# Output projection of layer 0 as seven half products per pair of column tiles, sums of weights added by DMA

## The chip, the cores and the metric

The kernel runs on one core of a Trainium2 chip. The metric is the device time of one execution in microseconds (us). Three runs of the kernel before are shown, and one further execution of it was taken by the hardware profiler; the profile and the trace quoted below are of that one.

## The reference

A trunk of two layers over 512 tokens and 16 meta tokens (528 in all, T in the code), width 2048, all in float32. Layer 0 is grouped-query attention, layer 1 gated linear attention. Each layer is `h <- h + post_norm(mixer(pre_norm(h)))`, with RMS norms over the width. What the change touches is the end of layer 0's mixer, then its post-norm and residual:

```
o = ...                                    # (528, 2048): 16 heads of 128
y = (o * silu(gate)) @ w_out               # 2048 x 2048: the output projection
h = h + rmsnorm(y, post_norm[0])
u = rmsnorm(h, pre_norm[1])                # input of layer 1's projections
```

## The kernel before

**Layout and precision.** Activations lie feature-major: a tile is 128 features by 528 tokens, `uh[:, k]` and `ul[:, k]` for k in 0..15. Every float32 operand is split in two parts: `split` (L130) makes the high part by a copy on ScalarE (ACT) and the rest by a subtraction on VectorE (DVE). A product of weights and activations is three matmuls, high*high, high*low and low*high (`three`, L153). Weights come by `weights` (L143): one DMA on SyncE's queue (SP) of 128 x 1024 elements into one of two buffers `wraw`, then the split into one of three pairs `whi`, `wlo`.

**Output projection of layer 0.** The gated heads `og` were written to DRAM (`og_d`) while attention ran; `reload` (L542) brings them back, splits them into `uh`, `ul`, and multiplies the last two by their gates. The first two column tiles run side by side with k outermost (`group`, L171), because heads arrive one by one; the other 14 run in `project` (L158, called at L682): 16 values of k for the first half of the tokens (264), then 16 for the second. That is 16 column tiles x 2 halves x 16 k x 3 = 1536 matmuls of 264 columns.

**What follows a tile.** `squares` (L601) lets ACT copy the result from PSUM to SBUF, scaled by the post-norm's weight, into `hs[m]`, which stays in SBUF, and square it; GpSimd (POOL) adds the square to `acc`. After the last tile `mean_rsqrt` (L618) makes the norm `r0` by a matmul with ones, for each half of the tokens. `residual` (L625) then forms the new `h` from `hs[k]`, `r0` and the old `h` (from DRAM, `h0_d`), and splits it into `uh`, `ul` for layer 1. The first half's norm is ready while the second half of the last tile still runs, so the residual starts before the projection ends. The first group of layer 1 (`group` with `low_rank`, L649) takes k as the residual delivers it.

**What sets the order.** The program is recorded through a scheduler; `tc.high_priority(n)` moves an instruction up. Each engine runs its own queue strictly in order. A tile from a pool with a given number of buffers waits until the last reader of the buffer's former tile is done, and the wait stands in the queue of the engine that writes it, in front of everything behind it.

Of the kernel before, what the change touches and what calls it, by code (L numbers as in the profile page):

```python
# [19 lines left out]
P = 128  # L20
# [14 lines left out]
AHEAD = 400  # L35
SLOTS = (2.8, 3.5, 3.5, 3.5, 3.5, 3.5, 3.5, 2.6)


class Clock:
    """Order of emission: main steps advance the time, events run when it has come."""  # L40
# [42 lines left out]
def hybrid_encoder(  # L83
# [37 lines left out]
    def col(i):  # L121
        return cols[:, i:i + 1]
# [3 lines left out]
    # the activations of both layers and their gated outputs, feature-major, in two parts  # L126
# [31 lines left out]
    def project(src, c0, parts, evac, last_k=None):  # L158
        """One column tile of a projection: all of k for one part of the tokens, then for the next."""
# [11 lines left out]
    def group(srcs, accs, extra, ahead=AHEAD, halves=0, units=None):  # L171
        """Several column tiles side by side, k outermost; the first of k by halves of the tokens, if asked."""
# [15 lines left out]

    w_in0 = attn_w_in[0].rearrange("(k p) n -> p k n", p=P)
# [5 lines left out]
    # ======== layer 0: attention ========  # L195
# [156 lines left out]
    # per-token sums of squares: the norm as a column, and along the tokens  # L352
# [182 lines left out]
    slots.append(wa.tile([P, T], F32, tag="vt", name="ogr", bufs=1))  # L535
    NS = len(slots)

    def load_og(k):
        if k < 14:
            nc.sync.dma_start(out=slots[k % NS], in_=og_d[k])  # L540

    def reload(k):  # L542
        if k < 14:
            og = slots[k % NS]
        else:
            if k == 14:
                clk.finish(att)
            og = o_sb[k - 14]
            V.tensor_tensor(og, og, last_gs[k - 14], op=ALU.mult)
        split(uh[:, k], ul[:, k], og)  # L550
        load_og(k + NS)

    for k in range(NS):
        load_og(k)
    EARLY = 4
    last_gs.append(gate(15, lambda k: reload(k - 10) if 10 <= k < 10 + EARLY else None))

    accs0, banks0 = [], []
    for m in range(2):
        for j, (a, b) in enumerate(HALVES):  # L560
            ps = (ps_t.tile([P, 512], F32, tag="t", name="po") if m and j else
                  ps_p.tile([P, 512], F32, tag="pp", name="pp"))[:, :b - a]
            accs0.append((ps, 0, m * P, a, b))
            banks0.append((m, ps, a, b))
# [3 lines left out]
    r1row = c1.tile([P, T], F32, name="r1row")  # L568
# [4 lines left out]
    qf = c1.tile([P, 2, SEQ], F32, name="qf")  # L573

# [1 line left out]
    tr = ExitStack()  # L576
    tp = pool(tr, "tp")
    t2 = pool(tr, "t2", 2)
    hs = [tp.tile([P, T], F32, name=f"h{k}") for k in range(KT)]
    acc = tp.tile([P, T], F32, name="acc")  # L580
    r0 = tp.tile([P, T], F32, name="r0")
    # low-rank gate weights: the down-projection as columns [f hi, b hi, f lo, b lo] from multiples of 32,
    # the up-projections as rows [hi, lo, hi] against the inputs' rows [hi, hi, lo]
# [17 lines left out]
    def squares(m, ps, a, b):  # L601
        A.activation(hs[m][:, a:b], ps, AF.Copy, scale=col(POST + m))
        if m == 0:
            A.activation(acc[:, a:b], ps, AF.Square)
            return
        sq = t2.tile([P, 512], F32, tag="sq", name="sq")[:, :b - a]
        A.activation(sq, ps, AF.Square)
        if m < KT - 1:
            G.tensor_tensor(acc[:, a:b], acc[:, a:b], sq, op=ALU.add)
        return sq  # L610

    for m, ps, a, b in banks0:
        squares(m, ps, a, b)
    ps0.close()
    ps_g = pool(tr, "ps_g1", space=PSUM)
    ps_t = pool(tr, "ps_t1", space=PSUM)

    def mean_rsqrt(row, parts, a, b):  # L618
        ps = ps_t.tile([P, 512], F32, tag="t", name="ssq")[:, :b - a]
        for i, p in enumerate(parts):  # L620
            PE.matmul(ps, ones, p, start=(i == 0), stop=(i == len(parts) - 1))
        V.tensor_scalar(row[:, a:b], ps, 1.0 / D, EPS, op0=ALU.mult, op1=ALU.add)
        rsqrt_inplace(row[:, a:b])

    def residual(k, a, b):  # L625
        if a == 0:
            h0s[k] = t2.tile([P, T], F32, tag="h0", name="h0", bufs=6)
            nc.sync.dma_start(out=h0s[k], in_=h0_d[k])
        h, hi = hs[k][:, a:b], uh[:, k, a:b]
        V.tensor_tensor(h, h, r0[:, a:b], op=ALU.mult)  # L630
        (G if k % 2 else V).tensor_tensor(h, h, h0s[k][:, a:b], op=ALU.add)
# [439 lines left out]
```

## Time and profile before

| | |
|---|---|
| Time, three runs | 1827.38 us median (1826.25 to 1829.39) |
| Span of the profiled execution, first to last instruction | 1825.2 us |
| Median time less that span (start and end around it) | 2.2 us |
| TensorE matmul (PE) busy | 1784.4 us, 98% |
| VectorE (DVE), ScalarE (ACT), GpSimd (POOL) busy | 56%, 49%, 11% |
| Mean granted TensorE clock | 0.995 of full speed |
| Moved by DMA | 184.22 MB |

The profile's page gives the span by engine, by time slices, the chain of work that ended last, and groups of instructions by source line with their count and mean time. The trace can be asked for one tile or one stretch of time. "PE idle" below always means that TensorE had no matmul under way. The output projection takes about 755 to 943 us of the span; the residual with the first group of layer 1 lies from 940 to 1000 us.

### The profile page before, as it was taken

The numbers are of one execution on the slowest core, as the hardware profiler recorded it, in microseconds if no ns is written. First come the engines' busy times: TensorE is split into PE (matmuls) and PEld (weight loads), VectorE is DVE, ScalarE is ACT, GpSimd is POOL, SyncE is SP. The second block draws the span as 40 slices with busy tenths as digits, with TensorE's granted clock in tenths as the row PEclk, the third lists the DMA queues.
The fourth block names the chain that finished last, engine by engine and source line by source line (L and its number), as shares of the span: only waits on it lengthen the run. The fifth ranks groups of instructions, "written<-read, shape, count | busy, mean of one in ns | idle before, by whom it ended". The sixth has DMA issues, their size and how long they took to land.

```text
span 1825.2 us, 31789 instructions
## 1 busy us (share of the span) xinstructions
PE 1784.4 (98%) x12825; PEld 1683.3 (92%) x12825; DVE 1014.2 (56%) x1941; ACT 892.9 (49%) x1835; POOL 202.5 (11%) x212
## 2 busy tenths in 40 slices
PE   8899999999999999999987999999999999999997
PEld 7899999999999999999987898998999899988886
DVE  5776665656565657622258475656456555654224
ACT  5555444454454544533245586556447455743221
POOL 2211111111111110211137000000000000000000
PEclk9999999999999999999998999999999999999999
DMA  8323232333223242633335323232232323434323
GB/s 266 106 59 82 82 88 85 93 85 88 83 87 93 81 120 76 185 93 93 93 88 163 87 72 89 83 82 82 81 93 80 84 87 92 134 116 172 94 92 127
DMA packets 264595, 184.22 MB, mean 101 GB/s; under 512 B 8108, under 2 KB 240112, under 8 KB 263920
## 3 DMA queue, kind: packets, MB, share of 16 engines
q1 hardware_dynamic: 259808, 165.78, 31.5%
q0 software_dynamic: 4640, 16.42, 2.5%
q8 instruction: 100, 1.64, 0.4%
q14 instruction: 47, 0.39, 0.1%
HBM read 156.03 MB, written 19.64 MB: 96 GB/s over the span
## 4 chain that ended last, share of the span: by engine, by line
PE 92%; DVE 3%; ACT 1%; DMA 1%; POOL 1%; issue 1%; SPq 0%; DVEq 0%; POOLq 0%; ACTq 0%
PE pp L154 22%; PE pp L156 22%; PE pp L155 22%; PE f L985 2%; PE f L983 2%; PE f L984 2%; PE pT L453 2%; PE s L434 1%; PE s L435 1%; PE s L436 1%; PE o L863 1%; PE o L862 1%; PE o L861 1%; PE o L474 1%; PE o L473 1%
## 5 line engine op out<-in xcount | busy, mean ns | idle before, releaser
L154 PE MATMUL pp<-uh,whi 128*128 128x264 f32 (+1 forms) x3072 | 927.4, 302 | 2.5 <-ACT uh L308 2.1
L156 PE MATMUL pp<-uh,wlo 128*128 128x264 f32 (+1 forms) x3072 | 916.4, 298 | 0.0
L155 PE MATMUL pp<-ul,whi 128*128 128x264 f32 (+1 forms) x3072 | 915.1, 298 | 0.7 <-DVE ul L309 0.7
L154 PEld LDWEIGHTS pp<-uh,whi 128*128 128x128 f32 x3072 | 578.5, 188 | 21.1 <-ACT uh L308 2.5
L155 PEld LDWEIGHTS pp<-ul,whi 128*128 128x128 f32 x3072 | 578.8, 188 | 16.9 <-DVE ul L309 1.2
L156 PEld LDWEIGHTS pp<-uh,wlo 128*128 128x128 f32 x3072 | 578.5, 188 | 16.2
L132 DVE TENSOR_TENSOR wlo<-wraw,whi 128x1024 fp32r<-128x1024 f32 x256 | 316.0, 1235 | 385.8 <-ACT whi L131 380.7
L131 ACT CAST whi<-wraw 128x1024 fp32r<-128x1024 f32 x256 | 267.7, 1047 | 416.1 <-PE pp L155 297.1
L443 ACT ACTIVATE pn<-s,mx 128x528 f32<-128x528 f32 (+1 forms) x72 | 50.4, 699 | 88.4 <-DVE mx L440 65.0
L985 PE MATMUL f<-whi,ul 128*128 128x512 f32 x192 | 75.6, 394 | 0.0
L983 PE MATMUL f<-whi,uh 128*128 128x512 f32 x192 | 75.5, 393 | 0.0
L984 PE MATMUL f<-wlo,uh 128*128 128x512 f32 x192 | 75.3, 392 | 0.0
L225 POOL TENSOR_TENSOR qw<-qw,cos 128x528 f32<-128x528 f32 x24 | 31.9, 1328 | 372.2 <-DMA qs<-qw 347.7
L888 POOL DMA_DIRECT2D og_d<-og x24 | 12.9, 545 | 486.8 <-DVE og L886 486.8
L439 DVE TENSOR_REDUCE mx<-s 128x1 f32<-128x528 f32 (+1 forms) x72 | 50.8, 705 | 18.5 <-PE s L436 17.3
L235 DVE TENSOR_TENSOR qw<-qw,qs 128x528 f32<-128x528 f32 x24 | 17.0, 708 | 60.0 <-POOL qs L226 60.0
L458 DVE TENSOR_TENSOR pl<-pT,ph 128x512 fp32r<-128x512 f32 (+1 forms) x80 | 47.4, 593 | 4.8 <-ACT ph L457 3.8
L457 ACT CAST ph<-pT 128x512 fp32r<-128x512 f32 (+1 forms) x80 | 40.7, 508 | 16.5 <-PE pT L453 10.4
L428 POOL TENSOR_TENSOR gs<-gs,gr 128x528 f32<-128x528 f32 x16 | 21.2, 1323 | 222.3 <-ACT gs L141 205.4
L984 PEld LDWEIGHTS f<-wlo,uh 128*128 128x128 f32 x192 | 36.1, 188 | 8.3
L985 PEld LDWEIGHTS f<-whi,ul 128*128 128x128 f32 x192 | 36.1, 188 | 8.3
L983 PEld LDWEIGHTS f<-whi,uh 128*128 128x128 f32 x192 | 36.1, 188 | 8.1
(306 smaller groups left out, 2743.2 us busy)
## 6 DMA issues: line engine op xcount, KB each, us to landing
wraw<-in_gla_w_in_dram SPq DMA_DIRECT2D x96, 512.0 KB, 3.9
wraw<-in_attn_w_in_dram SPq DMA_DIRECT2D x95, 512.0 KB, 4.1
wraw<-in_attn_w_out_dram SPq DMA_DIRECT2D x32, 512.0 KB, 3.9
wraw<-in_gla_w_out_dram SPq DMA_DIRECT2D x32, 512.0 KB, 3.8
qs<-qw SPq DMA_DIRECT2D x96, 66.0 KB, 3.0
h<-h_d SPq DMA_DIRECT2D x16, 264.0 KB, 3.8
h_d<-h POOLq DMA_DIRECT2D x16, 256.0 KB, 2.9
h_d<-hb SPq DMA_DIRECT2D x16, 256.0 KB, 3.1
```

The lines of the kernel that those rows point to most:

```text
L131: A.copy(hi, src)
L132: V.tensor_tensor(lo, src, hi.bitcast(F32), op=ALU.subtract)
L154: PE.matmul(ps, wh, uh[:, k, a:b], start=first, stop=False)
L155: PE.matmul(ps, wh, ul[:, k, a:b], start=False, stop=False)
L156: PE.matmul(ps, wl, uh[:, k, a:b], start=False, stop=last)
L439: V.reduce_max(mx, s, axis=AX.XY)
L443: A.activation(pn[:, :T].rearrange("p (a b) -> p a b", a=2), s, AF.Exp, bias=mx, scale=SCALE, accum_out=sm)
L457: A.copy(ph[:, :, c:c + m], pt[:, :, qc:qc + m])
L458: V.tensor_tensor(pl[:, :, c:c + m], pt[:, :, qc:qc + m], ph[:, :, c:c + m].bitcast(F32), op=ALU.subtract)
L983: PE.matmul(ps, uh[:, k, ts], wh[:, kk], start=(k == 0), stop=False)
L984: PE.matmul(ps, uh[:, k, ts], wl[:, kk], start=False, stop=False)
L985: PE.matmul(ps, ul[:, k, ts], wh[:, kk], start=False, stop=(k == KT - 1))
```

## The change

Column tiles are taken in pairs. With the weights of a pair as a 2 x 2 block matrix (A: column tile by half of k, 8 tiles each) and the activations as one (B: half of k by half of the tokens), the eight half products of a pair become seven, each of 8 values of k and 264 tokens (`product`). Numbers of the products are P1 to P7 in `pair_products`.

- **Sums of weights.** `Pair` loads four 128 x 1024 blocks by SP. Four more blocks are added onto the loaded ones by accumulating DMAs that POOL issues (`accum_op=ALU.add`): `chain` is A21, then A21+A22 for P5, then +A11 for P6, then +A12 for P3; `a11` becomes A11+A21 for P7. `chain` and `a11` have six buffers `sraw` together.
- **Sums of activations.** `sums_of(j)`, for 8 values of j, reloads two heads (`o1`, `o2`) from `og_d`, forms four sums on POOL (`d0` to `d3` in the built program) and splits five blocks. `o1` and `o2` share two buffers; each `d` has one.
- **Order.** P1 of the pairs 0 to 3 comes first, on the first half of tokens, then P2 of these pairs beside the sums, then the rest pair by pair: five products for the pairs 0 to 3, seven for 4 to 7.
- **Output.** The pieces of y are combined by DVE, squared by ACT, the squares added by POOL, and each piece of 128 x 264 is written to DRAM (`y_d`) by a DMA that POOL issues. `residual` loads `hs[k]` back from `y_d` (10 buffers) and multiplies by the post-norm's weight itself.
- **Moved.** The small weights of layer 1 (`wr`, `ur`, `wl`, `ups`) were prepared at the projection's start and are now prepared at its end; the first six loads of `h0_d` too.

The diff, cut to its core:

```
+    def split_neg(hi, lo, src):
+        A.activation(hi, src, AF.Copy, scale=-1.0)
+        V.scalar_tensor_tensor(lo, src, -1.0, hi.bitcast(F32), op0=ALU.mult, op1=ALU.subtract)
...
+    class Pair:
+        def __init__(self, src, c0, rawp, ahead=2 * AHEAD):
+            def load(i, j, t, q=nc.sync, **kw):
+                c = c0 + i * P
+                q.dma_start(out=t.rearrange("p (k n) -> p k n", n=P), in_=src[:, 8 * j:8 * j + 8, c:c + P], **kw)
+            def add(i, j, t):
+                with tc.high_priority(ahead):
+                    load(i, j, t, G, accum_op=ALU.add)
...
+                self.chain, self.a11 = [rawp.tile([P, 1024], F32, tag="sraw", name="sraw", bufs=RAWS) for _ in range(2)]
+                self.a12, self.a22 = [wpool.tile([P, 1024], F32, tag="wraw", name="wraw", bufs=2) for _ in range(2)]
+                load(1, 0, self.chain)
+                load(0, 0, self.a11)
+                load(0, 1, self.a12)
+                load(1, 1, self.a22)
+                load(1, 1, self.chain, G, accum_op=ALU.add)
+        def weights(self, n):
+            if n == 7:
+                self.add(1, 0, self.a11)
+            if n == 6:
+                self.add(0, 0, self.chain)
+            if n == 3:
+                self.add(0, 1, self.chain)
+            return split_w({1: self.a11, 7: self.a11, 2: self.a12, 4: self.a22}.get(n, self.chain))
+    def product(w, u):
+        (wh, wl), (bh, bl) = w, u
+        ps = ps_p.tile([P, 512], F32, tag="pp", name="pp")[:, :HALF]
+        for k in range(8):
+            PE.matmul(ps, wh[:, k], bh[:, k], start=(k == 0), stop=False)
+            PE.matmul(ps, wh[:, k], bl[:, k], start=False, stop=False)
+            PE.matmul(ps, wl[:, k], bh[:, k], start=False, stop=(k == 7))
...
-    group([(w_out0, 0, 256)], accs0, lambda k, _: reload(k) if k >= EARLY else None)
...
-    for m in range(2, KT):
-        project(w_out0, m * P, HALVES, evac)
...
+    so2 = pool(so, "so2", 2, side="right")
+    def sums_of(j):
+        o1 = so2.tile([P, T], F32, tag="og", name="o1")
+        o2 = so2.tile([P, T], F32, tag="og", name="o2")
+        nc.sync.dma_start(out=o1, in_=og_d[j])
+        nc.sync.dma_start(out=o2, in_=og_d[j + 8])
+        (b11, b12), (b21, b22) = [[o[:, a:b] for a, b in HALVES] for o in (o1, o2)]
+        d1, d2, d3, d4 = [so2.tile([P, HALF], F32, tag=f"d{i}", name=f"d{i}", bufs=1) for i in range(4)]
+        G.tensor_tensor(d1, b12, b11, op=ALU.subtract)
+        G.tensor_tensor(d2, d1, b22, op=ALU.subtract)
+        G.tensor_tensor(d3, b22, b12, op=ALU.subtract)
+        G.tensor_tensor(d4, d2, b21, op=ALU.add)
+        split(B22[0][:, j], B22[1][:, j], b22)
+        split_neg(T1[0][:, j], T1[1][:, j], d1)
+        split(T2[0][:, j], T2[1][:, j], d2)
+        split(T3[0][:, j], T3[1][:, j], d3)
+        split_neg(T4[0][:, j], T4[1][:, j], d4)
...
+    def done(m, j, first=False, last=None):
...
+            A.activation(sq, y, AF.Square)
+            G.tensor_tensor(acc[:, a:b], acc[:, a:b], sq, op=ALU.add)
...
+        nc.gpsimd.dma_start(out=y_d[m][:, a:b], in_=y)
...
+            hs[k] = t2.tile([P, T], F32, tag="hk", name="hk", bufs=10)
+            nc.sync.dma_start(out=hs[k], in_=y_d[k])
...
-        V.tensor_tensor(h, h, r0[:, a:b], op=ALU.mult)
+        V.scalar_tensor_tensor(h, h, col(POST + k), r0[:, a:b], op0=ALU.mult, op1=ALU.mult)
...
+    def pair_products(i, last):
+        pr = Pair(w_out0, 2 * i * P, so2)
+        if i >= NX:
+            take_p1(i, product(pr.weights(1), B11))
+            take_c11(i, product(pr.weights(2), B21))
+        u2, u3, u4, p5 = [so2.tile([P, HALF], F32, tag=f"u{n}", name=f"u{n}", bufs=1) for n in (2, 3, 4, 5)]
+        A.copy(p5, product(pr.weights(5), T1))
+        V.tensor_tensor(u2, product(pr.weights(6), T2), p1s[i], op=ALU.add)
+        V.tensor_tensor(u4, u2, p5, op=ALU.add)
+        ps = product(pr.weights(7), T3)
...
+        ps = product(pr.weights(4), T4)
...
+        ps = product(pr.weights(3), B22)
```

**Where instructions moved.** First GpSimd's queue at the projection's start. Names: `gs` is the last head's gate, `wr`, `wl`, `ur`, `lr`, `ups` the small weights of layer 1, `acc` the sum of squares. Before:

```order
L428 TENSOR_TENSOR gs_9492<-gs_9492,gr_9367 128x528
L585 DMA wr_9786<-in_gla_w_in_dram 128x16x32
L587 MEMSET wl_9788 128x2048
L591 DMA ur_9794<-in_gla_gk_up_dram 16x2x1024
L593 MEMSET lr0_9757 80x528
L593 MEMSET lr1_9758 80x528
L593 MEMSET ups_9759 80x2048
L609 TENSOR_TENSOR acc_9784<-acc_9784,sq_9810 128x264
```

The same place now, from the last of six accumulating DMAs (`sraw` from the weights) on; `sraw_10001` is the chain of pair 0, `y` a piece of the output, and `d0` to `d3` the four sums, with a new set of numbers for each j:

```order
L214 DMA sraw_10372<-in_attn_w_out_dram 128x8x128
L707 DMA y_d_9653<-y_9746 128x264
L659 TENSOR_TENSOR d0_9697<-o1_9693 128x264
L707 DMA y_d_9653<-y_9823 128x264
L660 TENSOR_TENSOR d1_9698<-d0_9697,o2_9694 128x264
L661 TENSOR_TENSOR d2_9699<-o2_9694,o1_9693 128x264
L662 TENSOR_TENSOR d3_9700<-d1_9698,o2_9694 128x264
L214 DMA sraw_10001<-in_attn_w_out_dram 128x8x128
L659 TENSOR_TENSOR d0_9752<-o1_9748 128x264
L707 DMA y_d_9653<-y_9900 128x264
L707 DMA y_d_9653<-y_9977 128x264
L660 TENSOR_TENSOR d1_9753<-d0_9752,o2_9749 128x264
```

The small weights left this place; accumulating DMAs, stores and sums share one queue. The accumulation of A11 onto pair 0's chain stands between the sums of j = 0 and j = 1.

Second, SyncE's queue in the same stage (`h0` is the old h, `ogr` a reloaded head). Before:

```order
L149 DMA wraw_9684<-in_attn_w_out_dram 128x4x256
L540 DMA ogr_9357<-og_d_70 128x528
L540 DMA ogr_9358<-og_d_70 128x528
L149 DMA wraw_9832<-in_attn_w_out_dram 128x8x128
L540 DMA ogr_9359<-og_d_70 128x528
L540 DMA ogr_9360<-og_d_70 128x528
L149 DMA wraw_9838<-in_attn_w_out_dram 128x8x128
L628 DMA h0_11461<-h0_d_69 128x528
```

Now, with `o1`, `o2` of j = 0 to 3 and the raw weights between them:

```order
L655 DMA o1_9693<-og_d_70 128x528
L656 DMA o2_9694<-og_d_70 128x528
L214 DMA wraw_10003<-in_attn_w_out_dram 128x8x128
L655 DMA o1_9748<-og_d_70 128x528
L214 DMA wraw_10004<-in_attn_w_out_dram 128x8x128
L214 DMA wraw_10186<-in_attn_w_out_dram 128x8x128
L656 DMA o2_9749<-og_d_70 128x528
L214 DMA wraw_10187<-in_attn_w_out_dram 128x8x128
L655 DMA o1_9770<-og_d_70 128x528
L214 DMA sraw_10558<-in_attn_w_out_dram 128x8x128
L656 DMA o2_9771<-og_d_70 128x528
L655 DMA o1_9825<-og_d_70 128x528
```

In the built program each `o1` waits for `d2` of the j before it, and each `o2` for `d3` of the j before it.

Third, GpSimd's queue later in the projection, where before it held nothing but these:

```order
L609 TENSOR_TENSOR acc_9784<-acc_9784,sq_9894 128x264
L609 TENSOR_TENSOR acc_9784<-acc_9784,sq_9947 128x264
L609 TENSOR_TENSOR acc_9784<-acc_9784,sq_10012 128x264
L609 TENSOR_TENSOR acc_9784<-acc_9784,sq_10065 128x264
L609 TENSOR_TENSOR acc_9784<-acc_9784,sq_10130 128x264
```

Now, around the end of pair 1 (`sraw_10184` its chain) and the start of pair 2 (`sraw_10371` its chain; `sraw_10745` is the chain of pair 4):

```order
L214 DMA sraw_10184<-in_attn_w_out_dram 128x8x128
L214 DMA sraw_10745<-in_attn_w_out_dram 128x8x128
L707 DMA y_d_9653<-y_10290 128x264
L702 TENSOR_TENSOR acc_9639<-acc_9639,sq_10292 128x264
L702 TENSOR_TENSOR acc_9639<-acc_9639,sq_10327 128x264
L214 DMA sraw_10371<-in_attn_w_out_dram 128x8x128
L707 DMA y_d_9653<-y_10325 128x264
```

A store and two additions now stand ahead of the DMA that adds A11 onto pair 2's chain.

More of the change, by code (lines that the diff above doesn't have):

```diff
@@ L35 @@
 AHEAD = 400
+RAWS = 6
 SLOTS = (2.8, 3.5, 3.5, 3.5, 3.5, 3.5, 3.5, 2.6)
@@ L558, in hybrid_encoder @@
[L558 to L564, printed above, removed]
-    group([(w_out0, 0, 256)], accs0, lambda k, _: reload(k) if k >= EARLY else None)
-    l0.close()
+        load_a(k)
+    last_gs.append(gate(15, lambda k: reload_a(k - 2) if 2 <= k < 10 else None))
@@ new lines, in hybrid_encoder, with piece, take_p1, take_c11 @@
+    p1s, ys = {}, {}
+    def piece():
+        return so2.tile([P, HALF], F32, tag="y", name="y", bufs=NX + 6)
+    def take_p1(i, ps):
+        p1s[i] = so2.tile([P, HALF], F32, tag="p1", name="p1", bufs=NX)
+        A.copy(p1s[i], ps)
+    def take_c11(i, ps):
+        ys[2 * i, 0] = piece()
+        V.tensor_tensor(ys[2 * i, 0], ps, p1s[i], op=ALU.add)
+    todo0 = list(range(8))
+    for i in range(3):
+        take_p1(i, early[i])
+    for i in range(3, NX):
+        take_p1(i, product(half_weights(2 * i, 0), B11))
+        sums_of(todo0.pop(0))
```

177 lines of the change are left out of this document (109 added, 68 removed).

## The prediction

> **What bounds the kernel now.** First the page: busy time by engine, and the chain of work that ended last.
>
> ```profile
> PE 1784.4 (98%) x12825; PEld 1683.3 (92%) x12825; DVE 1014.2 (56%) x1941; ACT 892.9 (49%) x1835; POOL 202.5 (11%) x212
> ...
> PE 92%; DVE 3%; ACT 1%; DMA 1%; POOL 1%; issue 1%; SPq 0%; DVEq 0%; POOLq 0%; ACTq 0%
> ```
>
> TensorE is the bound nearly everywhere, and GpSimd is the emptiest engine. Next, windows of 20 us inside the output projection and of 5 us in the residual behind it; the columns are named in the first row, clock and DMA share last.
>
> ```profile
> core 0: us, PE busy (x) PEld busy (x) DVE busy (x) ACT busy (x) POOL busy (x), PEclk, DMA share, GB/s
> 780.00:800.00 20.00, 20.00 (x167) 20.00 (x166) 3.12 (x4) 6.37 (x13) 4.11 (x5) 1.00 0.28 80
> ...
> 950.00:955.00 5.00, 2.73 (x19) 2.17 (x17) 5.00 (x9) 3.21 (x8) 3.57 (x5) 1.00 0.28 69
> ...
> 990.00:995.00 5.00, 1.97 (x9) 1.76 (x10) 5.00 (x4) 3.13 (x6) 4.53 (x4) 0.69 0.09 26
> 995.00:1000.00 5.00, 5.00 (x30) 5.00 (x29) 3.27 (x3) 2.27 (x4) 4.39 (x6) 0.63 0.56 152
> 1000.00:1005.00 5.00, 5.00 (x44) 5.00 (x43) 0.00 (x0) 1.18 (x2) 0.00 (x0) 1.00 0.66 194
> ```
>
> In the projection PE never stops: 167 matmuls of 264 columns in 20 us, 0.1198 us each, while every other engine and the DMA are mostly idle. In the residual DVE is full and PE waits. Last, the two ends of the stage in the timeline: the evacuation of the last gate, and the last matmul of the projection with the first one on layer 1's data.
>
> ```profile
> 755.37 0.43 DVE L425 TENSOR_TENSOR gr<-pp,rrow 128x264 f32<-128x264 f32 x1
> ...
> 939.96 0.78 DVE L630 TENSOR_TENSOR h<-h,r 128x264 f32<-128x264 f32 x2 [0.95 <-ACT r L136]
> ...
> 942.29 0.28 PE L156 MATMUL pp<-uh,wlo 128*128 128x264 f32 x1
> 942.70 0.39 PE L652 MATMUL plr<-uh,wl 128*128 128x264 f32 x1
> ```
>
> The projection has PE for itself from 755.3 to 942.6, and layer 1 follows without a gap, because the residual (L630) begins 2.6 us before the projection ends.
>
> **The matmuls removed.** Eight pairs x 7 products x 8 k x 3 are 1344 matmuls instead of 1536, all still 128 x 128 by 264. 192 x 0.1198 = **23.0 us saved**, since PE is never idle here. One product takes 24 x 0.1198 = 2.88 us.
>
> **The sums of activations.** The rows for this part: GpSimd's 264-column addition, its DMA issues, the load of a head, and the weight split with its load.
>
> ```profile
> L609 POOL TENSOR_TENSOR acc<-acc,sq x28: 742/757/1131, 780.5 to 931.7; 128x264 f32<-128x264 f32 x28
> ...
> 759.02 1.32 POOL L428 TENSOR_TENSOR gs<-gs,gr 128x528 f32<-128x528 f32 x1 [11.76 <-ACT gs L141]
> ...
> L525 POOL DMA_DIRECT2D og_d<-o_sb x14 | 8.2, 583 | 14.6 <-DVE o_sb L524 7.3 <-DVE sm L444 6.3 <-DVE pl L458 1.0
> L585 POOL DMA_DIRECT2D wr<-in_gla_w_in_dram x1 | 1.2, 1216 | 0.0
> L149 POOL DMA_DIRECT2D wraw<-in_attn_w_in_dram x1 | 0.8, 806 | 0.0
> ...
> L540 SPq DMA_DIRECT2D ogr<-og_d x14: 319/320/386, 648.6 to 759.1; - x14
> ...
> DMA to landing us min/median/max: 2.7/4.1/5.7
> ...
> L131 ACT CAST whi<-wraw x32: 1037/1047/1048, 755.1 to 939.8; 128x1024 fp32r<-128x1024 f32 x32
> L132 DVE TENSOR_TENSOR wlo<-wraw,whi x31: 1219/1226/1227, 756.3 to 931.0; 128x1024 fp32r<-128x1024 f32 x31
> L149 SPq DMA_DIRECT2D wraw<-in_attn_w_out_dram x28: 367/368/383, 757.6 to 917.6; - x28
> ...
> DMA to landing us min/median/max: 3.6/3.9/5.6
> ...
> wr<-in_gla_w_in_dram POOLq DMA_DIRECT2D x1, 256.0 KB, 5.2
> h<-h_d POOLq DMA_DIRECT2D x4, 1024.0 KB, 8.2
> h_d<-h POOLq DMA_DIRECT2D x16, 256.0 KB, 2.9
> ```
>
> The eight P1 and P2 that run beside the sums last 23.0 us, to 755.3 + 23.0 = 778.3. The sums form a chain: `o2` of one j may load only when `d3` of the j before has read its buffer; then `d1`, `d2`, `d3` follow on GpSimd. One link is 2.7 to 4.1 us of landing (I take 3.4, since SP carries little else then), 3 x 0.76, and 0.2 for two semaphores: 5.9 us. GpSimd alone needs 4 x 0.76 = 3.0 us for each j, 24 us for eight, so the 23 us of cover would not do even without loads.
>
> Step by step. GpSimd finishes the last gate's store at 763.8 and then issues six accumulating DMAs. Their issue I put at 0.9 us, between 0.81 and 1.22 of the two rows with short runs. `o1`, `o2` of j = 0 stand behind the weights of the last P2, which wait for the split of the P2 two before: P1 of pair 3 ends at 766.8, its copy and that split end at 769.5, the heads land at 774.3. `d3` of j = 0 ends at 777.7. Then GpSimd adds A11 onto pair 0's chain; an accumulating DMA is not in the trace, and I take 5.2 us to landing as in the `wr` row, also a GpSimd load of many short runs (bounds 3.9, the same block loaded by SP, and 8.2, the longest GpSimd load): 783.8. GpSimd's next accumulation waits for the split of that chain (2.3 us) and so does the rest of j = 1, whose `d3` ends at 787.8. A raw load and its accumulation stand before j = 2: 794.5. Four links of 5.9 give 818.1 for j = 6; `o2` of j = 7 lands at 821.6, its T2 is split at 823.2. P5, P6 and P7 of pair 0 take each k as it comes (PE's queue interleaves them), and T3 of j = 7 waits behind the split for P3: P7 ends at 826.8. Without waits it would end at 778.3 + 8.6 = 786.9: **40 us lost**. With 2.7 us for each load and 3.9 for the accumulation it is 33, with 4.1 and 8.2 and additions at 0.95 it is 49; none of the links can fall away, so a gain is excluded.
>
> **The accumulations of the later pairs.** P6 uses the chain after A11 was added, which may start only when the split for P5 has read it, and that needs a weight buffer freed three products before P5. From there: split 2.3 us, issue 0.9, landing 5.2, split 2.3 and 0.1 are 10.8; PE arrives at the first low part after three products and two matmuls, 8.9. So each pair waits landing - 3.3 = 1.9 us, and pairs 1 to 7 lose 13.3. In pairs 2 and 3 a store (0.55) and two additions (1.5) stand ahead in GpSimd's queue, some 1.6 us more each. For P3's accumulation there are, from P6's third matmul to P3's, 8.6 - 0.9 - 2.3 = 5.4 us to land, so it is hidden at 5.2. **16.5 us lost**; at a landing of 3.9 it is 7.4, at 8.2 it is 37.5 and P3 adds 2.8 x 7: 57.
>
> On this price the Trainium skill speaks, DMA: Bandwidth & Descriptors, section "Anatomy of one DMA": a GpSimd-issued DMA takes about 2.0 us plus its bytes over 436 GB/s. By it 512 KB land in an estimated 3.2 us, the links above would all but hide, and the sum would be some 14 us lower. The rows above (5.2 us for 256 KB, 8.2 for 1 MB) are slower than that rule; it is the second rival.
>
> Of other work, splits and pieces stay hidden: seven splits of 1.05 us on ACT and 1.23 on DVE in 20.2 us. If all eight blocks and stores of a pair (4.7 MB) moved at 288 GB/s, what queue 1's 165.78 MB in 31.5% of the span amounts to, they would take 16 us against 14.4 to 20.2; here too a slow accumulation would bind.
>
> ```profile
> q1 hardware_dynamic: 259808, 165.78, 31.5%
> ```
>
> **The end of the projection.** Rows: the small weights prepared by ACT and DVE, and the norm.
>
> ```profile
> L594 ACT CAST ups<-ur 16x2048 fp32r<-16x2048 f32 x1 | 1.9, 1909 | 0.0
> L596 DVE TENSOR_TENSOR ups<-ur,ups 16x2048 fp32r<-16x2048 f32 x1 | 2.3, 2282 | 0.7 <-ACT ups L594 0.7
> L622 DVE TENSOR_SCALAR r<-ssq 128x264 f32<-128x264 f32 x2 | 0.9, 426 | 6.4 <-PE ssq L621 6.4
> ```
>
> The first `hs[k]` is no longer in SBUF. Its load waits in SP's queue for the store of P4's last piece: 0.45 (DVE) + 0.55 (issue) + 2.9 (landing) + 3.4 (load) = 7.3 us after P4, 4.4 after P3, where before the residual began 2.6 us ahead of the end. That is 7 us later, and DVE's stage behind it is as long as before: two weight splits (2.5) come earlier, `ups` (2.3) comes in. ACT's two copies of 1.9 us stand around the first residual tiles, 0 to 2 us. **8 us lost**, 5 if the load has landed early, 14 if the later loads from `y_d`, behind the stores of `hb` (layer 1's transposed copy of h), keep DVE waiting.
>
> **The clock.** Rows 990 to 1000 show 0.69 and 0.63 granted once PE is mostly idle, and 1.00 again 5 us later. The sums leave PE idle for four fifths of 48 us, so some 5 us behind them run at about 0.65: **2 us** (0 to 4). The Trainium skill, TensorE: Matmul & The Clock Gate, section "Part 1", says that an idle window of about 3.4 us halves the clock until another 3.4 us were busy; by that it is an estimated 1.7 us, and the rows agree in kind.
>
> **Sum.** -23.0 + 40 + 16.5 + 8 + 2 = +43.5 us. On the span of 1825.2 that gives 1868.7, and with the 2.2 us around it, which the median of the runs shows, **1871 us**. All low ends give 1850, all high ends 1928.
>
> **Rivals.**
> - *Sums covered (faster).* If loads of the next j overlapped GpSimd's work and GpSimd kept pace with PE, the sums would cost nothing: -23.0 + 7.4 + 8 = -7.6, 1820 us. It decides at a link of 2.9 us; GpSimd's four operations alone take 3.0, and the waits in the built program put the load into each link. For it speaks only that the trace shows no GpSimd this busy. 5%.
> - *Accumulations no dearer than a load.* At the 3.9 us of the same block loaded by SP the pairs lose 7.4 instead of 16.5 us and the sums 1.3 less: 1861 us. For it speaks that both move the same 1024 short runs, against it the slower GpSimd rows. 17%. The rule of the Trainium skill named above (DMA: Bandwidth & Descriptors) would make it some 4 us less still.
> - *Slow accumulations.* If adding means that each engine reads two streams, landing is 8 us or more and the DMA engines are full; pairs lose 57 instead of 16.5, sums 3 more: about 1914. It decides from a landing of 5.4 on, where P3 waits too. 15%.
> - *A wash.* Short links and hidden accumulations together still leave 1850, so within 0.2% needs a mistake in the chain: 2%.
>
> That the saving itself is not there is excluded: PE's queue holds the fewer matmuls.
>
> **Numbers.** The forecast, sums at 33 to 49 with accumulations at about 5 us, has 61%. The range 1846 to 1900 takes it in with the second rival and half of what lies between it and the third, leaving out the faster case and the slow accumulations' end. 0.2%, about 4 us, is what measurements of this kernel can tell from no change. Faster 5%, same 2%, slower 93%.
>
> **What would show it.** Right: PE mostly idle from about 778 to 825, with GpSimd's `d` operations about 6 us apart and waiting for DMA `o2`; then a wait of 2 us before P6 in each pair, ended by the split of the chain; residual work that starts 4 us after the last product. Wrong: landing of `sraw` far from 5 us, loads of `o2` that land before `d3` of the j before ends, or PE idle under 25 us in the sums.

## The result

| | before | after |
|---|---|---|
| Time, median of 4 runs, us | 1827.01 (1826.25 to 1829.39) | 1942.43 (1941.2 to 1943.53) |
| Ratio | | 1.0627, 95% interval 1.0612 to 1.0642 |
| Span of the profiled execution, us | 1825.2 | 1941.2 |
| Mean granted clock | 0.995 | 0.962 |
| Moved by DMA, MB | 184.22 | 216.84 |

The change is slower, as forecast, but by 115 us instead of 43.5; 1942 lies outside the range of 1846 to 1900.

### The profile page after: what moved, and what is told of

It reads as the page before. It is cut to its first block, busy times and chain, and to the rows that moved or that the text cites. A ratio compares the mean times of both kernels' runs of the same rounds, so it can differ in the third digit from the quotient of the medians.

```text
span 1941.2 us, 31974 instructions
## 1 busy us (share of the span) xinstructions
PE 1809.5 (93%) x12637; PEld 1693.0 (87%) x12637; DVE 1091.2 (56%) x2061; ACT 921.0 (47%) x1883; POOL 294.5 (15%) x308
## 2 busy tenths in 40 slices
DMA packets 314550, 216.84 MB, mean 112 GB/s; under 512 B 9804, under 2 KB 286608, under 8 KB 313872
## 3 DMA queue, kind: packets, MB, share of 16 engines
q1 hardware_dynamic: 274784, 176.73, 31.7%
q0 software_dynamic: 39616, 38.06, 9.9%
## 4 chain that ended last, share of the span: by engine, by line
PE 77%; DMA 8%; DVE 5%; issue 3%; POOL 3%; ACT 2%; SPq 1%; DVEq 0%; POOLq 0%; ACTq 0%
PE pp L155 17%; PE pp L157 17%; PE pp L156 17%; DMA sraw<-in_attn_w_out_dram 6%; PE f L1128 2%; PE f L1126 2%; PE f L1127 2%; PE pT L514 2%; DVE wlo L133 1%; ACT whi L132 1%; DMA o<-og_d 1%; PE s L495 1%; PE s L496 1%; PE s L497 1%; DVE ul L726 1%
## 5 line engine op out<-in xcount | busy, mean ns | idle before, releaser
L155 PE MATMUL pp<-uh,whi 128*128 128x264 f32 (+1 forms) x2576 | 786.7, 306 | 5.1 <-ACT uh L369 4.8
L157 PE MATMUL pp<-uh,wlo 128*128 128x264 f32 (+1 forms) x2576 | 775.4, 301 | 0.0
L156 PE MATMUL pp<-ul,whi 128*128 128x264 f32 (+1 forms) x2576 | 774.6, 301 | 0.5 <-DVE ul L370 0.5
L155 PEld LDWEIGHTS pp<-uh,whi 128*128 128x128 f32 x2576 | 485.1, 188 | 23.5 <-ACT uh L369 5.2
L156 PEld LDWEIGHTS pp<-ul,whi 128*128 128x128 f32 x2576 | 485.5, 188 | 16.5 <-DVE ul L370 0.8
L157 PEld LDWEIGHTS pp<-uh,wlo 128*128 128x128 f32 x2576 | 485.1, 188 | 16.4
L244 PE MATMUL pp<-uh,whi 128*128 128x264 f32 x256 | 77.5, 303 | 29.1 <-ACT whi L132 16.9
L133 DVE TENSOR_TENSOR wlo<-sraw,whi 128x1024 fp32r<-128x1024 f32 x36 | 48.7, 1371 | 80.1 <-ACT whi L132 80.0
L246 PE MATMUL pp<-uh,wlo 128*128 128x264 f32 x256 | 76.6, 299 | 3.3 <-DVE wlo L133 3.2
L245 PE MATMUL pp<-ul,whi 128*128 128x264 f32 x256 | 76.7, 300 | 1.8 <-DVE ul L199 1.7
L214 POOL DMA_DIRECT2D sraw<-in_attn_w_out_dram x32 | 50.7, 1596 | 81.4 <-DVE wlo L133 47.5
```

Source lines behind the costliest of these rows:

```text
L133: V.tensor_tensor(lo, src, hi.bitcast(F32), op=ALU.subtract)
L155: PE.matmul(ps, wh, uh[:, k, a:b], start=first, stop=False)
L156: PE.matmul(ps, wh, ul[:, k, a:b], start=False, stop=False)
L157: PE.matmul(ps, wl, uh[:, k, a:b], start=False, stop=last)
L214: q.dma_start(out=t.rearrange("p (k n) -> p k n", n=P), in_=src[:, 8 * j:8 * j + 8, c:c + P], **kw)
L244: PE.matmul(ps, wh[:, k], bh[:, k], start=(k == 0), stop=False)
```

## The profile after

The page of the changed kernel: busy time by engine, the two DMA queues that carry most of the data (q1 holds what SP issues, q0 what GpSimd issues; packets, MB, share of 16 engines' span), and the chain of work that ended last.

```profile
PE 1809.5 (93%) x12637; PEld 1693.0 (87%) x12637; DVE 1091.2 (56%) x2061; ACT 921.0 (47%) x1883; POOL 294.5 (15%) x308
...
q1 hardware_dynamic: 274784, 176.73, 31.7%
q0 software_dynamic: 39616, 38.06, 9.9%
...
PE 77%; DMA 8%; DVE 5%; issue 3%; POOL 3%; ACT 2%; SPq 1%; DVEq 0%; POOLq 0%; ACTq 0%
```

TensorE is busier in microseconds with fewer matmuls, because many of them ran at a lower clock, and DMA now has 8% of the chain. Next the windows of 20 us that answer to 780 to 800 of before, in the columns named there.

```profile
780.00:800.00 20.00, 8.29 (x45) 7.56 (x45) 4.16 (x4) 3.88 (x5) 6.24 (x6) 0.66 1.23 221
...
820.00:840.00 20.00, 10.21 (x30) 6.84 (x28) 9.40 (x15) 5.60 (x14) 10.64 (x12) 0.50 0.71 142
...
900.00:920.00 20.00, 14.60 (x110) 13.88 (x109) 6.87 (x10) 6.43 (x10) 7.89 (x10) 0.93 0.92 167
...
940.00:960.00 20.00, 13.73 (x93) 12.79 (x91) 5.59 (x7) 5.21 (x6) 3.70 (x3) 0.83 0.97 164
```

TensorE stands still in all three parts of the projection: at its start, in the sums of activations, and in the pairs. The DMA share, the time of all packets over the time of 16 engines, is 1.23 at the start and 0.92 to 0.97 in the pairs. It can pass 1, where packets of one engine overlap in time, so 1 is no bound.

All 1344 matmuls are in the trace, so the loss can be placed. Call a matmul late by the time from the first matmul's start, less its number times 0.1198 us. The changed kernel's matmuls are late by 24.0 us after eight products, by 74.2 when P7 and P4 of pair 0, which PE's queue interleaves, have ended, and by 132.4 at the end. With the 23.0 us saved and a start 0.8 us earlier that leaves a remainder of 7.4 us of the 116.0 between the spans. Where TensorE stood still, the trace gives what it waited for; the rest of the lateness is matmuls that took longer than 0.1198 us. These two parts are 83 and 49 us.

**The start.** SP's queue, weights of P1 and P2 (L150) among the blocks of the pairs (L214), then ACT, which splits them.

```profile
754.64 0.38 SPq L150 DMA_DIRECT2D wraw<-in_attn_w_out_dram  x1
755.08 6.74 SPq L214 DMA_DIRECT2D sraw<-in_attn_w_out_dram  x4
761.86 4.01 SPq L150 DMA_DIRECT2D wraw<-in_attn_w_out_dram  x2
765.91 5.75 SPq L214 DMA_DIRECT2D sraw<-in_attn_w_out_dram  x2
772.45 9.44 SPq L150 DMA_DIRECT2D wraw<-in_attn_w_out_dram  x2
```

```profile
770.12 1.04 ACT L132 CAST whi<-wraw 128x1024 fp32r<-128x1024 f32 x1 [6.43 <-DMA wraw<-in_attn_w_out_dram]
...
791.11 1.04 ACT L132 CAST whi<-wraw 128x1024 fp32r<-128x1024 f32 x1 [12.25 <-DMA wraw<-in_attn_w_out_dram]
```

Six blocks and six accumulations of the first three pairs go out among the weights that the next product needs. The last row holds two loads and a short pause between them: the two issues take 4.3 and 3.8 us, where 0.37 is usual, each load lands 18 us after its issue began, and ACT waits 12 us for one.

**The sums.** GpSimd's queue; the columns behind the time are duration and, in brackets, the wait ahead of it.

```profile
834.31 0.74 POOL L659 TENSOR_TENSOR d<-o 128x264 f32<-128x264 f32 x1 [1.90 <-DMA o<-og_d]
...
837.06 0.93 POOL L662 TENSOR_TENSOR d<-d,o 128x264 f32<-128x264 f32 x1
840.01 0.74 POOL L659 TENSOR_TENSOR d<-o 128x264 f32<-128x264 f32 x1 [2.02 <-DMA o<-og_d]
...
845.55 0.74 POOL L659 TENSOR_TENSOR d<-o 128x264 f32<-128x264 f32 x1 [1.91 <-DMA o<-og_d]
```

One link of the chain is 5.6 us: additions, then 2 us of waiting for the next heads.

**A pair.** GpSimd's accumulations on one chain (A11 at 997.23, then A12 at 1007.21) with what stands ahead of them, an accumulation of the next pair and additions of squares, and ACT's splits of that chain for P6 and P3.

```profile
992.00 1.60 POOL L214 DMA_DIRECT2D sraw<-in_attn_w_out_dram  x1
...
994.81 2.42 POOL L702 TENSOR_TENSOR acc<-acc,sq 128x264 f32<-128x264 f32 x1
997.23 1.62 POOL L214 DMA_DIRECT2D sraw<-in_attn_w_out_dram  x1
...
1007.21 1.58 POOL L214 DMA_DIRECT2D sraw<-in_attn_w_out_dram  x1 [7.78 <-DVE wlo L133]
```

```profile
1004.61 1.99 ACT L132 CAST whi<-sraw 128x1024 fp32r<-128x1024 f32 x2 [9.37 <-DMA sraw<-in_attn_w_out_dram]
...
1013.91 1.05 ACT L132 CAST whi<-sraw 128x1024 fp32r<-128x1024 f32 x1 [6.09 <-DMA sraw<-in_attn_w_out_dram]
```

Three steps in series, 7.4 + 2.6 + 6.7 us, and then the second split: the first accumulation lands, its split reads the chain, the second lands. The trace counts landing from the start of the issue, so the 1.6 us of the issue lie inside the 7.4. The product whose end freed the weight buffer for P5's split ended at 991.92; the first accumulation is issued 5.3 us later. The issue groups of the stage (750 to 1060 us) give the landing, last column:

```profile
q0 software_dynamic: 35104, 22.04, 48.1%
...
sraw<-in_attn_w_out_dram POOLq DMA_DIRECT2D x32, 512.0 KB, 8.3
wraw<-in_attn_w_out_dram SPq DMA_DIRECT2D x21, 512.0 KB, 6.8
```

Of these 32 accumulations the first six, at the start, land after 10.9 to 20.9 us; the seven ahead of P6 in the pairs 1 to 7 after 6.3 to 8.6, in the median 7.1.

**The end.** SP's queue, then DVE, then the first matmul on layer 1's data:

```profile
1035.80 17.48 SPq L150 DMA_DIRECT2D wraw<-in_gla_w_in_dram  x4
1053.46 0.45 SPq L719 DMA_DIRECT2D hk<-y_d  x1
```

```profile
1057.67 0.90 DVE L723 SCALAR_TENSOR_TENSOR hk<-hk,cols,r 128x264 f32<-128x264 f32 x2 [4.10 <-DMA hk<-y_d]
```

```profile
1059.73 0.57 PE L816 MATMUL plr<-uh,wl 128*128 128x264 f32 x1
```

The last product ends at 1047.95. DVE has other work until 1053.57 and then stands idle for 4.1 us until the first `hk` lands, whose load is issued at 1053.46. Layer 1's first matmul starts 11.8 us after the last product; before, it started 0.1 us after. So the end itself costs 11.7 us. The remainder of 7.4 is smaller for two reasons: the kernel before needed 187.4 us for its projection (755.2 to 942.6), 3.4 more than 1536 x 0.1198, and 0.9 us are won back later.

## Experiments

Theory A: the accumulating DMAs were mis-sized, because adding is dearer than loading. Rivals: B, the price is that of GpSimd's queue, adding or not; C, the pairs wait for buffers and splits whatever the DMAs do. The table gives the lateness after the first products, after P7 and P4 of pair 0, and at the end, from each trace. The first of these is taken where the next product starts, so it holds the wait ahead of that product. The kernel before, run beside each group of experiments, had medians of 1826 to 1829 us, so small differences are better read from the ratios.

| run | ratio to before (95% interval) | first products | P7 and P4 of pair 0 | end |
|---|---|---|---|---|
| changed kernel | 1.0627 (1.0612 to 1.0642) | 24.0 | 74.2 | 132.4 |
| no sums of weights | 1.0177 (1.0162 to 1.0192) | 8.4 | 49.7 | 52.6 |
| DMAs without adding | 1.0419 (1.0402 to 1.0436) | 14.7 | 65.8 | 94.3 |
| sums on VectorE | 1.0224 (1.0209 to 1.0239) | 28.8 | 50.7 | 59.9 |
| four raw buffers | 1.0574 (1.0559 to 1.0590) | 20.4 | 57.4 | 121.0 |
| filled wait | 1.0643 (1.0617 to 1.0669) | 24.9 | 74.9 | 136.9 |
| P4 ahead of P6 | 1.0667 (1.0642 to 1.0692) | 23.7 | 69.0 | 143.5 |
| blocks later | 1.0564 (1.0547 to 1.0582) | 11.6 | 59.0 | 120.7 |
| no A12 | 1.0545 (1.0517 to 1.0572) | 24.4 | 73.9 | 122.3 |
| filled wait, no A12 | 1.0512 (1.0490 to 1.0534) | 23.5 | 73.5 | 115.0 |
| VectorE, 8 pairs first | 1.0140 (1.0124 to 1.0156) | 16.6 | 31.3 | 44.4 |
| the same, 4 head buffers | 1.0143 (1.0127 to 1.0159) | 30.6 | 30.7 | 47.6 |
| VectorE and GpSimd, 6 pairs first | 1.0175 (1.0160 to 1.0190) | 34.7 | 39.6 | 52.0 |

The first products are eight, in the last three rows 16, 16 and 12.

**No sums of weights.** The accumulating DMAs go, and P3, P5, P6 and P7 get unsummed blocks.

```
-                load(1, 1, self.chain, G, accum_op=ALU.add)
...
-            if n == 7:
-                self.add(1, 0, self.a11)
-            if n == 6:
-                self.add(0, 0, self.chain)
-            if n == 3:
-                self.add(0, 1, self.chain)
```

> The 32 accumulating DMAs are left out, so the sums of weights are missing (each product splits the block as loaded). Theory A, the accumulations are what was mis-sized: the 24 us lost over the first eight products and most of the 58 us lost after pair 0's P7 go, the sums of activations (about 42 us) and the end (about 11 us) stay: 1865 us (1855 to 1880). Theory C, the pairs wait for weight buffers and the split's own chain whatever the DMAs do: within 15 us of 1942.

1860.45 us. The accumulating DMAs cost 82 us of the 115; theory C falls. The rest of the change is still 32 us slower than before; of what it loses, 41 us lie in the sums of activations, 8 in the first products and 3 in the later pairs.

**The same DMAs, not adding.** Each overwrites its block, so the sums are missing.

```
-                    load(i, j, t, G, accum_op=ALU.add)
+                    load(i, j, t, G)
```

> The same 32 GpSimd DMAs, without adding: each overwrites its block (the sums are wrong). Theory A, adding itself is dear, because the engines read the block in SBUF too: landing falls from 8.3 to about 5 us, the wait ahead of P6 from 5 to 2 us, the first eight products lose under 12 us: 1885 us (1870 to 1900). Rival B, the price is that of GpSimd's queue with 1024 short runs, adding or not: landing stays near 8 us and the time within 15 us of 1942.

1904.40 us, 38 us less than the changed kernel. The issue group of the stage and the queue, first from the stage's answer, then from the page, and last the queue from the page of the run without sums:

```profile
q0 software_dynamic: 6432, 22.04, 23.5%
...
sraw<-in_attn_w_out_dram POOLq DMA_DIRECT2D x32, 512.0 KB, 5.5
```

```profile
q0 software_dynamic: 10944, 38.06, 6.1%
```

```profile
q0 software_dynamic: 6336, 21.28, 3.2%
```

Landing is 5.5 us instead of 8.3, and the issue takes GpSimd 0.9 us instead of 1.6. The bytes are equal, but 39616 - 10944 = 28672 packets are gone, 896 for each DMA: against the 6336 packets without any of these DMAs one that adds has 1040, a plain one 144, which agrees with the 1024 short runs of a block against one packet for each of 128 partitions, and 16 more in both. q0 without these DMAs had 3.2% of 1858.1 us (59.5 us), so the packets of one plain DMA amount to (0.061 x 1901.7 - 59.5) / 32 = 1.8 us of all 16 engines, and those of one that adds to (0.099 x 1941.2 - 59.5) / 32 = 4.1 us. Many packets alone are not the price: one of an adding DMA takes 4.1 x 16 / 1040, some 63 ns, and one of q1, where SP's loads of the same blocks run, 0.317 x 1941.2 x 16 / 274784, some 36 ns. Why a packet that adds takes longer is not shown.

A holds for 38 of the 82 us; B as stated (landing near 8 us, 1942) falls. The other 44 are what the same DMAs cost without adding: 6 in the first products, 10 in the sums, 26 in the pairs. The runs do not divide them between GpSimd's queue, the traffic, and the wait for a block's last reader. The 1885 expected was missed; one part is that the waits in the pairs (14.5 us after pair 0) were followed by as much in slow matmuls (14.1).

**Sums on VectorE.** All four blocks loaded by SP; S5, S6, S7 and S3 by additions of 1024 columns. The first sums:

```
+            if n == 5:
+                self.add(s7, a11, a21)
+                self.add(a21, a21, a22)
+            if n == 6:
+                self.add(a11, a11, a21)
+            if n == 3:
+                self.add(a12, a12, a11)
```

> The four sums of a pair are made by VectorE from four loaded blocks, 1.22 us each, into buffers that no split of the same pair holds up (A11 takes S6, A12 takes S3). Theory A: as without the sums, plus up to 10 us: 1870 us (1860 to 1885). Rival D, VectorE becomes the bound of a pair (7 splits and 4 sums and the combinations, some 16 us of 20): the pairs lose 3 us and more each and the time is over 1890.

1868.89 us, as A expected. The pairs lose 9.2 us instead of 58.2, so a sum of weights is cheap where VectorE has room. At the start it has none: the ninth product, the first of pair 0's own, waits for a combination of a P2 on VectorE.

```profile
806.56 0.56 PE L246 MATMUL pp<-uh,whi 128*128 128x264 f32 x1 [16.42 <-DVE y L682]
```

These 16.4 us are more than half of the 28.8 in the table. Between 784 and 806 VectorE makes eight sums of weights, four splits of weights and several splits of sums of activations ahead of that combination. In total this cost little, 50.7 us against 49.7 without the sums after P7 and P4 of pair 0, which suggests that the sums of activations bind there in both runs.

**Four raw buffers** (`RAWS = 4`).

> Four raw weight buffers instead of six: at the start of the projection the blocks and accumulations of two pairs are moved instead of three. If the start is slow because those transfers crowd out the weights of P1 and P2, its loss falls from 24 us to about 16 and the time by 5 to 10 us, unless later pairs lose the same by loading later (then 1942 stays). If it is slow for another reason, the loss at product eight stays at 24.

1932.37 us. The start falls only to 20.4; the sums, with other transfers ahead of them, gain 13 us, and the pairs lose 5 of it again.

**Blocks later.**

```
-        def __init__(self, src, c0, rawp, ahead=2 * AHEAD):
+        def __init__(self, src, c0, rawp, ahead=300):
```

> The changed kernel with one number changed: the blocks of a pair and their accumulations are moved up by 300 instead of 800 places, so that fewer of them stand among the first products. If they crowd out the weights of P1 and P2, the loss at product eight falls from 24 us to 10 or less and the time to 1920 us (1908 to 1930). If the later pairs then wait for their blocks instead, or the start is slow for another reason, 1935 or more.

1930.92 us, at the border of the two cases. The loss halves, to 9.4 us at the end of product eight and 11.6 with the wait ahead of the next one: the crowding is shown to be a matter of what stands ahead in the queues. But only 11.5 us reach the end.

**P4 ahead of P6.**

```
+        ps4 = product(pr.weights(4), T4)
         V.tensor_tensor(u2, product(pr.weights(6), T2), p1s[i], op=ALU.add)
...
-        ps = product(pr.weights(4), T4)
+        ps = ps4
```

> The changed kernel with P4 between P5 and P6, so that the accumulation of A11 has 2.9 us more to land. If the wait is the landing of 8.3 us less the cover, it falls from 5 to 2 us and the slow clock behind it too: pairs 4 to 7 gain 3 to 5 us each, pairs 1 to 3 at most as much: 1922 us (1910 to 1930). If the DMA engines' own work is the limit (four loads and four accumulations take them some 22 us a pair), the wait only moves to another product: within 8 us of 1942.

1950.85 us, no gain, at the edge of the second case. TensorE's waits from 863 to 1049 us (total, times, longest), changed kernel and this one:

```profile
PE pp L244 <- ACT whi L132: 30.7, 10, 5.7
```

```profile
PE pp L244 <- DVE u L742: 22.4, 6, 5.7
PE pp L244 <- ACT whi L132: 16.6, 5, 5.7
```

P6 now waits 16.6 us, and P3, which did not wait before, 22.4 (26.4 with pair 7, which lies behind this stretch): the wait has moved and grown. That agrees with the two accumulations in series: what P6 no longer waits, P3 waits, since its accumulation starts only when P6's split has read the chain. Six waits are put down to a combination on DVE (L742). DVE's queue shows what held that:

```profile
1020.24 1.23 DVE L133 TENSOR_TENSOR wlo<-sraw,whi 128x1024 fp32r<-128x1024 f32 x1 [6.95 <-ACT whi L132]
1021.39 0.42 DVE L742 TENSOR_TENSOR u<-pp,p 128x264 f32<-128x264 f32 x1
```

The split of the chain stands ahead of it and waits 7 us for ACT, which waits for the accumulation.

**The wait filled.** 36 matmuls whose result is not used, between P5 and P6.

```
+            for n in range(36):
+                PE.matmul(fill, w5[1][:, 7], T1[0][:, n % 8], start=(n == 0), stop=(n == 35))
```

> The changed kernel with 36 idle matmuls (4.3 us, result unused) between P5 and P6 of pairs 1 to 7, where TensorE waits 4.7 us for the accumulation. If the matmuls behind a wait are slow because the clock fell during it, the clock stays up: 7 x 2.6 us less, 1924 us (1917 to 1930). If they are slow for another reason (the DMA traffic, say), 1942 or more.

1945.87 us, no gain, against the theory that the slow clock costs 2.6 us a pair on top of the wait. The waits of the same stretch:

```profile
PE pp L244 <- ACT whi L132: 9.6, 7, 3.4
```

P6's wait is down to 0.5 us at most, and new ones of 1.1 to 3.4 us stand before P3 of four pairs, where the changed kernel had none. At the full clock P6, P7 and P4 take 8.6 us; the second accumulation takes longer (2.6 + 6.7 us and its split, above). In the changed kernel the slow matmuls of P6 had covered that.

**No A12**, without and with the filled wait (P3's weights lack A12).

```
-            if n == 3:
-                self.add(0, 1, self.chain)
```

> The changed kernel without the third accumulation on the chain (A12 for P3; P3's weights lack it). Theory, a pair pays for landings in series and the slow clock behind the first wait hides the second landing: little is gained, 1937 us (1930 to 1942). Rival, the DMA engines' time is the limit of a pair: one of four accumulations less gives 3 us a pair and more, 1920 or less.

> The run before (no A12 on the chain) together with the 36 idle matmuls between P5 and P6 of pairs 1 to 7. If the clock's fall costs time as soon as no second landing hides it, the filled wait now gains some 2.5 us a pair against the run before: 1920 us (1912 to 1928). If filling gains nothing here either, the slow matmuls are not the clock's, or something else binds: 1935 or more.

1927.87 and 1920.38 us. Leaving out one of four accumulations gains 14.5 us, between the two cases: about 10 in the pairs and 3 behind the last product. If the DMA engines' time bound the pairs, each would have gained the 4.1 us of one accumulation; they gained 1 to 2. P6's wait fell from about 5 us to 2.6 to 3.3 in four pairs though landing there stayed at 8.0 (7.6 before); why is not settled. With the wait filled, slow matmuls after pair 0 cost 6 to 7 us instead of 23, so the low clock did come from standing still. (Of the 41.5 us lost there, 3.7 are waits and some 31 the fill itself.) The total gained 7.5 us, at the value of the first case, but the intervals overlap, so that this gain is not shown.

**Other orders.** Sums of weights off the DMA; P1 and P2 of eight or six pairs first, so that the sums of activations have more beside them.

```
-    NX = 4
+    NX = 8
...
+        done(2 * i, 0, i == 0)
```

> Sums of weights on VectorE as in the run before, P1 and P2 of all eight pairs first (C11 pieces are squared and stored at once), and the blocks of a pair loaded later. If the sums of activations only lacked cover, eight links of 5.7 us (45 us) now lie beside 16 products (46 us), and the crowded start is gone: loss after pair 0's P7 falls from 51 us to 5 to 15, the end still costs 8 us: 1825 us (1815 to 1840). Rival: the weights of 16 products and the heads crowd SyncE's queue, and P2s starve as before: 1850 us and more.

> The run before with four buffers for the reloaded heads instead of two (and five raw weight buffers instead of six). If the link of 5.7 us is load plus additions in turn, the load now overlaps, links fall to the 3.4 us of GpSimd's additions, and what the run before still lost in the sums goes: 0 to 10 us faster than that run, 1820 us (1810 to 1832). If GpSimd's stores and squares fill its queue there, no difference.

> No accumulating DMA: P1 and P2 of six pairs first, three buffers for the heads, S5 and S6 on VectorE, S7 and S3 on GpSimd (some 2.9 us each). If VectorE was what held the pairs in the run with eight pairs first (13 us lost there) and the DMA what held its sums, both ease: 1838 us (1828 to 1850). If GpSimd's two sums of weights delay the sums of activations, 1855 or more.

1854.12, 1855.02 and 1858.11 us: better than the changed kernel by 84 to 88 us, none as fast as before, and none near its likelier case. In the first of these runs the sums after the 16 products still lose 15 us. In the second, with four head buffers, they lose 0.1, but the first 16 products lose 30.6 instead of 16.6, so the loss moved. The longest wait in the second run, and then in the third, is again for a combination in VectorE's queue:

```profile
826.99 0.56 PE L247 MATMUL pp<-uh,whi 128*128 128x264 f32 x1 [8.02 <-DVE y L683]
```

```profile
815.90 0.56 PE L247 MATMUL pp<-uh,whi 128*128 128x264 f32 x1 [15.05 <-DVE y L683]
```

Ahead of that combination stand splits of the sums and sums of weights. With VectorE making the sums of weights, its queue at the start was a limit that none of the expectations named; no run took it away. VectorE also slows beside GpSimd. The two in the second of these runs:

```profile
778.83 0.98 DVE L134 TENSOR_TENSOR ul<-o,uh 128x264 fp32r<-128x264 f32 x1
779.73 0.97 DVE L200 SCALAR_TENSOR_TENSOR ul<-d,uh 128x264 fp32r<-128x264 f32 x1
780.62 0.42 DVE L134 TENSOR_TENSOR t2l<-d,t2h 128x264 fp32r<-128x264 f32 x1
```

```profile
778.58 0.94 POOL L664 TENSOR_TENSOR d<-o,o 128x264 f32<-128x264 f32 x1
779.48 0.93 POOL L665 TENSOR_TENSOR d<-d,o 128x264 f32<-128x264 f32 x1
```

A subtraction of 264 columns takes DVE 0.42 us alone and 0.97 while GpSimd adds.

## Why the prediction was wrong

| term | forecast | measured |
|---|---|---|
| matmuls removed | -23.0 | -23.0 |
| first eight products | not among the terms | +24.0 |
| sums, with the clock behind them | +42 | +50.2 |
| accumulations of the later pairs | +16.5 | +58.2 |
| end of the projection; measured: the remainder | +8 | +7.4 |
| start 0.8 us earlier | | -0.8 |
| sum | +43.5 | +116.0 |

The step that failed is the price of an accumulating DMA, "I take 5.2 us to landing as in the `wr` row", together with its issue of 0.9 us. It took 1.6 us to issue and landed in 8.3 us in the median, beyond the upper bound of 8.2. The value of 5.2 was right for another thing, a GpSimd load that does not add (issue 0.9, landing 5.5). No row of before showed an addition, and the page could not say that its packets take 4.1 us of all DMA engines instead of 1.8. Resting the likeliest case on a row that adds nothing, with the bound at the slowest plain load, was the error; the rival of slow accumulations had this price, with 15%.

This price is not the whole miss. The run whose DMAs do not add has the price that was forecast, and it took 1904.40 us, not 1871. So of the 71 us by which the forecast was exceeded, 38 are the price of adding. The other 33 lie beyond its terms. In that run the first eight products lose 14.7 us, for which the forecast had nothing, the sums 9 more than forecast, and slow matmuls behind the waits of the pairs 14.1, for which it had nothing either. The waits of the pairs themselves, 14.5 us there, are near the 16.5 forecast.

In the changed kernel the pairs lost 58.2 us, close to the 57 that the forecast had for a landing of 8.2, but by other parts. The forecast had 37.5 us before P6 and 20 before P3; measured are 36 us of waits, nearly all of them for the split for P6 and none for P3, and 22 of slow matmuls. The working for P6 was also not as forecast. "Landing - 3.3" counts the issue twice, since the landing of the rows starts with the issue. And the accumulations ahead of P6 landed in 7.1 us, not 8.3, but in the pairs 2 to 6 they were issued 4.7 to 7.4 us after the weight buffer came free, not 2.3 (3.9 in two of them). In the pairs 4 to 6 an accumulation of the next pair and additions stood ahead in GpSimd's queue, and beside these additions the low half of the split took VectorE 2.6 to 3.2 us instead of 1.2; in the pairs 2 and 3 ACT was still waiting for an accumulation of the pair before (8.3 and 7.4 us) when the buffer came free. That 8.3 - 3.3 gives 5.0, and that five of the seven waits are 4.6 to 5.7, is chance.

The rule of the Trainium skill, DMA: Bandwidth & Descriptors, section "Anatomy of one DMA", gave an estimated 3.2 us. The measurements disagree, for the plain DMA (5.5) and more for the adding one (8.3); both stood among other traffic.

The first products show what the DMAs do to others. The forecast let the eight P1 and P2 run without a wait, to 778.3, and the sums begin beside them. The six accumulations were counted for their issue on GpSimd, 0.9 us each (measured 1.6), and not for what they and their blocks do to the weights behind them. The products end at 801.6. Without the accumulations the loss there is 8.4 us, with later blocks 9.4.

The sums were right in kind: the link was forecast at 5.9 us and is 5.6, with the wait on `o` as described, though on `o1` rather than on `o2` alone. Without the accumulating DMAs the part costs 41.3 us, against the 42 forecast; the 9 us more come with these DMAs between the sums, adding or not (51.1 without adding).

The clock was forecast at 2 us. 49 us of the lateness are slow matmuls, but much of that lies where TensorE would have waited anyway: in the sums it takes each k as it comes, and in a pair the slow P6 covers the landing for P3. That the filled wait gained nothing shows it for the pairs of the changed kernel; for the sums it is read from the trace and was not tried. Windows of the changed kernel around one wait:

```profile
936.00:942.00 6.00, 6.00 (x51) 6.00 (x50) 2.00 (x2) 0.38 (x1) 4.32 (x5) 1.00 1.15 207
942.00:946.80 4.80, 0.23 (x2) 0.01 (x1) 0.00 (x0) 1.07 (x2) 0.00 (x0) 0.76 0.96 148
946.80:952.30 5.50, 5.02 (x24) 4.72 (x25) 3.50 (x3) 2.14 (x3) 1.57 (x1) 0.59 0.30 79
952.30:958.00 5.70, 5.70 (x50) 5.70 (x48) 0.87 (x2) 0.30 (x1) 1.56 (x1) 1.00 1.33 225
```

After 4.8 us without work the clock is at 0.59 for the 24 matmuls of one product, which take 5.5 us instead of 2.9.

The end costs 11.7 us instead of 8, inside the bounds of 5 to 14; that the remainder of 7.4 comes so near to 8 is chance. Another part stands in front than was forecast: `hk`'s load stands behind four weight loads of layer 1 in SP's queue as well as behind the stores. That was read from the trace and not tried.

## What to carry to other kernels

When an operation is missing from the trace of before, its nearest relative may miss just what is new in it; keep the upper bound open, and ask what it does to the traffic beside it as well as to its own waiter. Where two transfers hang on one buffer in turn, price them as one chain: here hiding the first, by other work or by another order, only showed the second. A fast algorithm of this kind needs more work around each matmul: a pair had seven weight blocks to split where the plain form has four, with sums made by DMA eight block transfers instead of four, and its sums need an engine that is free at that moment.

## What the runs showed of the hardware

- An accumulating DMA of 512 KB had 1040 packets, whose time amounts to 4.1 us of all 16 DMA engines; a plain one from the same queue had 144 and 1.8 us. It landed in 8.3 us against 5.5 (medians, among other traffic) and took GpSimd 1.6 us to issue against 0.9.
- A packet of an accumulating DMA took some 63 ns, one of SP's queue, where the same short runs are loaded, 36 on average.
- A wait of 4.8 us brought the granted clock down to 0.59 for the next 5.5 us.
- DVE's operations of 264 columns took 0.97 instead of 0.42 us while GpSimd was adding.
